# First SwiGLU of a two-layer backbone: both conditioning rows spread over the partitions by products with ones, and five column pairs streamed by row blocks instead of four plus one

## The chip, the cores and the metric

The kernel runs on one core of one Trainium2 chip. The metric is the device time of one execution in microseconds (us), as the median of several runs. The core has these engines: TensorE does matrix products (PE in the profile; PEld is its weight load), VectorE (DVE) and ScalarE (ACT) do elementwise work, GpSimd (POOL) does fills, and SyncE (SP) issues the transfers from HBM. Each engine works through its own instructions in the order that was fixed when the kernel was built, and waits on semaphores for the others.

## The reference, cut to what matters

The reference computes two layers of a diffusion backbone on 256 latent tokens and 256 context tokens, each of width 1024. What comes first, and what the change is about, is the half-step SwiGLU of layer 0, with modulation from a conditioning vector (`c` for the latent tokens, `c_ctx` for the context tokens):

```
def adaln(cond, w, b):
    mm = jax.nn.silu(cond) @ w + b
    ...
def modulate(z, g, shift, scale):
    return rmsnorm(z, g) * (1.0 + scale) + shift
def swiglu(h, wi, wo):
    a, u = jnp.split(h @ wi, 2, axis=-1)
    return (jax.nn.silu(a) * u) @ wo
x = x + 0.5 * m[2] * swiglu(modulate(x, norm_g[l, 0], m[0], m[1]), ffn1_wi[l], ffn1_wo[l])
ctx = ctx + 0.5 * mc[2] * swiglu(modulate(ctx, norm_g[l, 0], mc[0], mc[1]), ffn1_wi[l], ffn1_wo[l])
```

`wi` is 1024 x 5632, that is 22 pairs of column blocks of 128 (one block of the `a` half, one of the `u` half). All data are fp32.

## The kernel before, in words

**Two kinds of product.** Features lie on the partitions, tokens along the free axis, and the 1024 features are 8 row blocks `k`. A plain product multiplies fp32 weights with fp32 data as they come; it is recorded as two MATMUL instructions for each pair of 128x128 weights and 128x256 data. A split product (`product`, L323) takes weights and data as a high and a low part of type fp32r, and sums three cheaper MATMULs (L328, L329, L330). The split of the weights is made in `weight` (L139): a transfer into one of four buffers tagged `raw`, a copy to `hi` on ScalarE (L145), and a subtraction to `lo` on VectorE (L146).

**The start.** `run` (L532) loads the conditioning rows. The row of `c` comes as an array of 128 equal rows, 512 KB (`crow0`, L548), into `srow[0]`, and ScalarE applies Silu to it in place (L564). The row of `c_ctx` comes as a single row of 4 KB (`crow1`, L547); two products with a row of ones (L568), each of 1 partition x 128 by 1 partition x 512, spread it over the partitions in PSUM, and Silu takes it from there into `srow[1]` (L570). The small parameters come as `cols` (L550). All these are issued on SP's queue.

**The modulation vectors** are dot products on VectorE: `mod_load` (L156) brings 128 columns of `w_mod` as a 512 KB tile, and `mod_dot` (L166) multiplies it with `srow[s]` and sums along the free axis (L175), for stream `s` = 0 (latent) or 1 (context). In the start phase the tiles have names `w0` to `w7`, one buffer each.

**The streamed part.** `begin` (L602) computes the first `FIRST` = 4 pairs of column blocks for the latent tokens while the input is still arriving. `lead(k)` (L580) issues the load of `w_mod` for row block `k` and, for even `k`, 256 KB of `xT`; makes the dot product and the scale (L202); and scales the row block into `xf` on ScalarE (L588). For each `k` a 512 KB tile of `wi0k` goes into a `raw` buffer (L609), and eight plain products (L611) add into the eight PSUM banks, one for each block. `other(k)` (L598) does the same dot product for the context stream; `S1_AT` says after which `k`. ScalarE loads the table for logarithm and exponential (`log_exp_tables`, L229) after the Silus. Afterwards eight copies (L624) take the results to `early`.

**The pairs after it.** `ffn_two` (L378) goes on with pairs `nf` to 10 for the latent tokens alone. `early_weights` (L643) loads the next pair's weights; for the first `PLAIN` = 1 of these (pair 4) they stay as they are and `early_pair` (L651) uses plain products (L655), for pairs 5 to 10 they are split. `during(p)` (L627) puts the work on the context tokens beside the pairs: at `p == FIRST` the load of `ctxT` (1 MB, L630); then, two row blocks at a time, scaling (L635), squares (L636) and the split (L595, L596); at `p == FIRST + RS_AT` = 8 the inverse root mean squares of both streams (`rstd_tables`, L233, whose scratch is a `raw` buffer). The shift vectors (channel 0, 16 more dot products) are made in between by `step_mod` (L188) and finished in `second` (L660). Then pairs 0 to 10 of the context tokens follow (L421), then all the rest of the kernel.

**Order.** Each queue's order is that of the program, moved about by a list scheduler at build time, which estimates when each instruction is ready. `after` (L135) pins an instruction behind another on its engine.

Of the kernel before, what the change touches and what calls it, by code (L numbers as in the profile page):

```python
# [8 lines left out]
F32 = mybir.dt.float32  # L9
# [3 lines left out]
AF = mybir.ActivationFunctionType  # L13
ALU = mybir.AluOpType

D = 1024
# [22 lines left out]

FIRST = 4  # L40
PLAIN = 1
RS_AT = 4
S1_AT = (1, 2, 3, 4, 5, 6)
# [64 lines left out]
class Body:  # L108
# [423 lines left out]
    def run(self):  # L532
# [12 lines left out]
        self.srow = [self.t(cp, [128, D]), self.t(ap, [128, D])]  # L545
        crow = self.t(sp, [1, D])
        nc.sync.dma_start(crow, a["crow1"])  # L547
        nc.sync.dma_start(self.srow[0], a["crow0"])  # L548
        self.cols = self.t(cp, [128, NCOL])
        nc.sync.dma_start(self.cols, a["cols"])  # L550
        self.xs = [self.t(cp, [128, KB, T]), self.t(ap, [128, KB, T])]
# [11 lines left out]

        self.silu = nc.scalar.activation(self.srow[0], self.srow[0], AF.Silu)  # L564
        for i in (0, 1):
            ps = self.bank()
            c = slice(i * 512, (i + 1) * 512)
            nc.tensor.matmul(ps, row1, crow[:, c], start=True, stop=True)  # L568
            with self.after(self.silu):
                self.silu = nc.scalar.activation(self.srow[1][:, c], ps, AF.Silu)  # L570

# [30 lines left out]
        def begin(early):  # L602

            lead(0)
            tables.append(self.log_exp_tables())
            ps = [self.bank() for _ in range(2 * FIRST)]
            for k in range(KB):
                w = self.t(self.wp, [128, 1024], F32, "raw", self.raw_bufs)
                nc.sync.dma_start(w[:, :2 * FIRST * 128], a["wi0k"][k])  # L609
                for i in range(2 * FIRST):  # L610
                    nc.tensor.matmul(ps[i][:, :T], w[:, i * 128:(i + 1) * 128], xf[:, k, :],  # L611
                                     start=(k == 0), stop=(k == KB - 1))
                lead(k + 1)
                with self.after(tables[0] if k == 0 else None):
                    self.square(ss0, self.xs[0][:, k, :], k)
                if k % 2:
                    parts(Xs[0], xf, k - 1)
                if k in S1_AT:
                    other(k)
            for k in range(KB):  # L620
                if k not in S1_AT:
                    other(k)
            for i in range(2 * FIRST):
                nc.scalar.copy(early[i // 2][:, i % 2, :], ps[i][:, :T])  # L624
            return FIRST

# [16 lines left out]
        def early_weights(p):  # L643
            if p < FIRST + PLAIN:
                ws = [self.t(self.wp, [128, 1024], F32, "raw", self.raw_bufs) for _ in (0, 1)]
                for q in (0, 1):
                    nc.sync.dma_start(ws[q], a["wi0"][p, q])
                return ws
            return [self.weight(a["wi0"][p, q], 1024) for q in (0, 1)]

        def early_pair(p, ws, ps):  # L651
            for q in (0, 1):
                if p < FIRST + PLAIN:
                    for k in range(KB):
                        nc.tensor.matmul(ps[q][:, :T], ws[q][:, k * 128:(k + 1) * 128], xf[:, k, :],  # L655
                                         start=(k == 0), stop=(k == KB - 1))
                else:
                    self.product(ps[q], ws[q], Xs[0], T)

# [583 lines left out]
def _layout(x, c, ctx, c_ctx, w_mod, b_mod, norm_g, ffn1_wi, ffn1_wo, ffn2_wi, ffn2_wo, w_in, w_a2_f, b_a_f,  # L1243
# [5 lines left out]
    A["xT"], A["ctxT"] = fm(x[0]), fm(ctx[0])  # L1249
    A["crow0"] = np.broadcast_to(c, (128, D))  # L1250
    A["crow1"] = c_ctx.reshape(1, D)
    A["cols"] = np.concatenate([col(norm_g), col(b_mod), col(pool_scale), col(final_g), col(gla_g), col(b_a_f),
# [35 lines left out]
```

## Time and profile before

| | us |
|---|---|
| median of 3 runs (1151.28 to 1153.29) | 1152.44 |
| the profiled execution, whole | 1152.83 |
| its span in the trace | 1151.0 |
| TensorE busy | 1126.8 |
| VectorE busy | 932.8 |
| ScalarE busy | 585.5 |
| first block product (L611) starts at | 10.64 |

In the profile a row of the timeline gives the start, the time until the end, the engine, the line of the kernel, what is written and read, and how many instructions are merged; in brackets stands how long the engine had been idle and what ended that. In a table of windows each row gives, for a stretch of the span, its length, then for PE, PEld, DVE, ACT and POOL the busy time with the number of instructions that start in it, then the granted clock, the share of the transfer engines in use, and GB/s. Rows for SPq are issues of transfers, not the transfers themselves.

### The profile page before, as it was taken

The page shows a single profiled execution, that of the slowest core. Times are in us where ns is not written, and L with a number is a line of the kernel's source. Part 1 is how long each engine was busy: PE and PEld are TensorE (multiplying, and loading weights), DVE is VectorE, ACT ScalarE, POOL GpSimd, SP SyncE. Part 2 cuts the span into 40 slices and gives each one's busy share as a digit, 9 for nine tenths or more (in the row PEclk, how much of TensorE's full clock was granted, in tenths as well). Part 3 has the DMA queues.
Part 4 walks back from the last instruction along what each step waited for, and adds up shares of the span by engine and source line. Part 5 has one row for each costly group of instructions (what it writes and reads, how often), then busy time and mean ns, then how long its engine had stood idle before and what let it go on. Part 6 is the DMA issues. An engine that isn't in the chain of part 4 may idle for free.

```text
span 1151.0 us, 19523 instructions
## 1 busy us (share of the span) xinstructions
PE 1126.8 (98%) x7450; PEld 1020.5 (89%) x7450; DVE 932.8 (81%) x1633; ACT 585.5 (51%) x998; POOL 7.3 (1%) x30
## 2 busy tenths in 40 slices
PE   7999999999999999999999999999999999999997
PEld 5999988888888899877899998899999888988886
DVE  6899899788758788876999868899986889977664
ACT  4647645323234464665574445564444556566543
POOL 0000000000000100000000000000000000000000
PEclk9999999999999999999999999999999999999999
DMA  9867557667766535313669868868986863755562
GB/s 343 298 246 233 162 175 234 201 218 251 243 186 195 170 116 178 124 62 110 202 215 325 317 218 261 280 214 305 330 295 202 272 220 136 256 188 190 153 186 89
DMA packets 74543, 247.41 MB, mean 215 GB/s; under 512 B 8273, under 2 KB 8913, under 8 KB 74194
## 3 DMA queue, kind: packets, MB, share of 16 engines
q1 hardware_dynamic: 74450, 246.17, 64.6%
q8 instruction: 58, 0.95, 0.3%
q14 instruction: 35, 0.29, 0.1%
HBM read 245.09 MB, written 1.05 MB: 214 GB/s over the span
## 4 chain that ended last, share of the span: by engine, by line
PE 85%; DVE 8%; DMA 3%; ACT 2%; issue 1%; SPq 0%; DVEq 0%; ACTq 0%
PE t_mm L337 15%; PE t_mm L344 11%; PE t_mm L345 11%; PE t_mm L343 11%; PE t_mm L338 8%; PE t_mm L330 7%; PE t_mm L329 7%; PE t_mm L328 7%; PE t_mm L611 2%; DVE t_lo L146 2%; DVE t_junk L175 1%; ACT t_hi L145 1%; PE t_mm L991 1%; DMA t_raw<-wi0k 1%; PE t_mm L932 1%
## 5 line engine op out<-in xcount | busy, mean ns | idle before, releaser
L145 ACT CAST t_hi<-t_raw 128x1024 fp32r<-128x1024 f32 (+1 forms) x344 | 326.0, 950 | 375.3 <-PE t_mm L344 168.6
L146 DVE TENSOR_TENSOR t_lo<-t_raw,t_hi 128x1024 fp32r<-128x1024 f32 (+1 forms) x344 | 376.6, 1097 | 85.0 <-ACT t_hi L145 82.4
L330 PE MATMUL t_mm<-t_xA,t_lo 128*128 128x258 f32 (+1 forms) x912 | 259.7, 285 | 3.8 <-DVE t_lo L146 3.7
L328 PE MATMUL t_mm<-t_xA,t_hi 128*128 128x258 f32 (+1 forms) x912 | 260.0, 286 | 2.8 <-DVE t_x L953 1.7
L329 PE MATMUL t_mm<-t_xA,t_hi 128*128 128x258 f32 (+1 forms) x912 | 258.1, 283 | 0.1
L175 DVE CUSTOM_DVE_ANT_0 t_junk<-t_rawm,t_x 128x1024 bf16<-128x1024 f32 x142 | 181.7, 1280 | 25.2 <-DMA t_rawm<-wmod 24.4
L337 PE MATMUL t_mm<-t_g,t_hi 128*128 128x512 f32 x528 | 186.6, 398 | 0.0
L343 PE MATMUL t_mm<-t_xA,t_hi 128*128 128x256 f32 (+1 forms) x592 | 186.2, 315 | 0.0
L345 PE MATMUL t_mm<-t_xA,t_lo 128*128 128x256 f32 (+1 forms) x592 | 186.2, 315 | 0.0
L344 PE MATMUL t_mm<-t_xA,t_hi 128*128 128x256 f32 (+1 forms) x592 | 186.2, 315 | 0.0
L328 PEld LDWEIGHTS t_mm<-t_xA,t_hi 128*128 128x128 f32 x912 | 173.0, 190 | 7.4 <-DVE t_x L953 1.9
L330 PEld LDWEIGHTS t_mm<-t_xA,t_lo 128*128 128x128 f32 x912 | 172.7, 189 | 5.1 <-DVE t_lo L146 5.1
L329 PEld LDWEIGHTS t_mm<-t_xA,t_hi 128*128 128x128 f32 x912 | 172.7, 189 | 1.4 <-DVE t_xA L320 0.6
L338 PE MATMUL t_mm<-t_g,t_lo 128*128 128x256 f32 x528 | 148.1, 280 | 0.0
L337 PEld LDWEIGHTS t_mm<-t_g,t_hi 128*128 128x128 f32 x528 | 99.1, 188 | 23.8
L343 PEld LDWEIGHTS t_mm<-t_xA,t_hi 128*128 128x128 f32 x592 | 112.9, 191 | 6.9
L344 PEld LDWEIGHTS t_mm<-t_xA,t_hi 128*128 128x128 f32 x592 | 112.9, 191 | 6.9
L345 PEld LDWEIGHTS t_mm<-t_xA,t_lo 128*128 128x128 f32 x592 | 112.9, 191 | 6.8
L338 PEld LDWEIGHTS t_mm<-t_g,t_lo 128*128 128x128 f32 x528 | 99.7, 189 | 0.0
L337 PE MATMUL t_mm<-t_xA,t_hi 128*128 128x512 f32 x272 | 96.2, 400 | 0.0
L338 PE MATMUL t_mm<-t_xA,t_lo 128*128 128x256 f32 x272 | 75.7, 280 | 0.3 <-DVE t_lo L146 0.3
L343 PE MATMUL t_mm<-t_g,t_hi 128*128 128x512 f32 x176 | 68.5, 389 | 0.0
(244 smaller groups left out, 1351.6 us busy)
## 6 DMA issues: line engine op xcount, KB each, us to landing
t_raw<-wi SPq DMA_DIRECT2D x190, 512.0 KB, 4.6
t_rawm<-wmod SPq DMA_DIRECT2D x118, 512.0 KB, 4.6
t_raw<-wo SPq DMA_DIRECT2D x64, 384.0 KB, 3.6
t_raw<-wo SPq DMA_DIRECT2D x64, 320.0 KB, 3.3
t_raw<-win SPq DMA_DIRECT2D x18, 512.0 KB, 3.6
t_w<-wmod SPq DMA_DIRECT2D x16, 512.0 KB, 6.7
t_raw<-wmod SPq DMA_DIRECT2D x10, 512.0 KB, 4.3
t_raw<-wi0k SPq DMA_DIRECT2D x8, 512.0 KB, 6.6
```

Of the source, the lines that this page charges most:

```text
L145: nc.scalar.copy(hi[:, :n], raw[:, :n])
L146: self.mark = nc.vector.tensor_tensor(lo[:, :n], raw[:, :n], hi.bitcast(F32)[:, :n], op=ALU.subtract)
L175: self.nc.vector.tensor_tensor_reduce(out=junk, in0=w, in1=self.srow[s], scale=0.5 if half else 1.0, scalar=b, op0=ALU.mult, op1=ALU.add, ...
L328: nc.tensor.matmul(ps[:, :n], hi[:, c], X[:, 0, k, :n], start=(k == 0), stop=False)
L329: nc.tensor.matmul(ps[:, :n], hi[:, c], X[:, 1, k, :n], start=False, stop=False)
L330: nc.tensor.matmul(ps[:, :n], lo[:, c], X[:, 0, k, :n], start=False, stop=(k == KB - 1))
L337: nc.tensor.matmul(ps, hi, X.rearrange("p x t -> p (x t)"), start=first, stop=False)
L338: nc.tensor.matmul(ps[:, T:], lo, X[:, 0], start=False, stop=last)
L343: nc.tensor.matmul(ps, hi, X0, start=first, stop=False)
L344: nc.tensor.matmul(ps, hi, X1, start=False, stop=False)
L345: nc.tensor.matmul(ps, lo, X0, start=False, stop=last)
L611: nc.tensor.matmul(ps[i][:, :T], w[:, i * 128:(i + 1) * 128], xf[:, k, :], start=(k == 0), stop=(k == KB - 1))
```

## The change

The row of `c` no longer comes as 128 equal rows. Both rows come as one row of 2 x 1024 numbers (`crow`, 8 KB, one transfer), and four products with ones spread them, the first two for `srow[0]`, the last two for `srow[1]`, each followed by a Silu on ScalarE in that order. `cols` is issued on ScalarE's queue instead of SP's.

`FIRST` becomes 5 and `PLAIN` disappears: pair 4 joins the streamed part, and all pairs after it are split. The ten blocks go two to a PSUM bank, so five banks are used, and five copies of 128x512 take the results. The weights of one `k` now need two `raw` buffers: one load of 1024 columns (512 KB), one of 256 columns (128 KB). `RS_AT` becomes 3, so the inverse root mean squares stay at pair 8; the `ctxT` load moves from pair 4 to pair 5.

```diff
-FIRST = 4
-PLAIN = 1
-RS_AT = 4
+FIRST = 5
+RS_AT = 3
...
-        crow = self.t(sp, [1, D])
-        nc.sync.dma_start(crow, a["crow1"])
-        nc.sync.dma_start(self.srow[0], a["crow0"])
+        crow = self.t(sp, [1, 2 * D])
+        nc.sync.dma_start(crow, a["crow"])
         self.cols = self.t(cp, [128, NCOL])
-        nc.sync.dma_start(self.cols, a["cols"])
+        nc.scalar.dma_start(self.cols, a["cols"])
...
-        self.silu = nc.scalar.activation(self.srow[0], self.srow[0], AF.Silu)
-        for i in (0, 1):
+        self.silu = None
+        for i in range(4):
             ps = self.bank()
-            c = slice(i * 512, (i + 1) * 512)
-            nc.tensor.matmul(ps, row1, crow[:, c], start=True, stop=True)
+            nc.tensor.matmul(ps, row1, crow[:, i * 512:(i + 1) * 512], start=True, stop=True)
             with self.after(self.silu):
-                self.silu = nc.scalar.activation(self.srow[1][:, c], ps, AF.Silu)
+                self.silu = nc.scalar.activation(self.srow[i // 2][:, i % 2 * 512:i % 2 * 512 + 512], ps, AF.Silu)
...
-            ps = [self.bank() for _ in range(2 * FIRST)]
+            ps = [self.bank() for _ in range(FIRST)]
             for k in range(KB):
-                w = self.t(self.wp, [128, 1024], F32, "raw", self.raw_bufs)
-                nc.sync.dma_start(w[:, :2 * FIRST * 128], a["wi0k"][k])
+                ws = [self.t(self.wp, [128, 1024], F32, "raw", self.raw_bufs) for _ in (0, 1)]
+                nc.sync.dma_start(ws[0], a["wi0k"][k, :, :1024])
+                nc.sync.dma_start(ws[1][:, :2 * FIRST * 128 - 1024], a["wi0k"][k, :, 1024:])
+                ins = None
                 for i in range(2 * FIRST):
-                    nc.tensor.matmul(ps[i][:, :T], w[:, i * 128:(i + 1) * 128], xf[:, k, :],
-                                     start=(k == 0), stop=(k == KB - 1))
+                    with self.after(ins if k == 0 else None):
+                        ins = nc.tensor.matmul(ps[i // 2][:, i % 2 * T:i % 2 * T + T],
+                                               ws[i // 8][:, i % 8 * 128:i % 8 * 128 + 128], xf[:, k, :],
+                                               start=(k == 0 and i % 2 == 0), stop=(k == KB - 1), skip_group_check=True)
...
-            for i in range(2 * FIRST):
-                nc.scalar.copy(early[i // 2][:, i % 2, :], ps[i][:, :T])
+            for e, p in zip(early, ps):
+                nc.scalar.copy(e.rearrange("p q t -> p (q t)"), p)
...
         def early_weights(p):
-            if p < FIRST + PLAIN:
-                ws = [self.t(self.wp, [128, 1024], F32, "raw", self.raw_bufs) for _ in (0, 1)]
-                for q in (0, 1):
-                    nc.sync.dma_start(ws[q], a["wi0"][p, q])
-                return ws
             return [self.weight(a["wi0"][p, q], 1024) for q in (0, 1)]
 
         def early_pair(p, ws, ps):
             for q in (0, 1):
-                if p < FIRST + PLAIN:
-                    for k in range(KB):
-                        nc.tensor.matmul(ps[q][:, :T], ws[q][:, k * 128:(k + 1) * 128], xf[:, k, :],
-                                         start=(k == 0), stop=(k == KB - 1))
-                else:
-                    self.product(ps[q], ws[q], Xs[0], T)
+                self.product(ps[q], ws[q], Xs[0], T)
...
-    A["crow0"] = np.broadcast_to(c, (128, D))
-    A["crow1"] = c_ctx.reshape(1, D)
+    A["crow"] = np.concatenate([c.reshape(1, D), c_ctx.reshape(1, D)], 1)
```

## The prediction, made before the result was known

> **What bounds the kernel now.** First the page: who is busy, and which engine the chain runs on.
>
> ```profile
> span 1151.0 us, 19523 instructions
> PE 1126.8 (98%) x7450; PEld 1020.5 (89%) x7450; DVE 932.8 (81%) x1633; ACT 585.5 (51%) x998; POOL 7.3 (1%) x30
> PE 85%; DVE 8%; DMA 3%; ACT 2%; issue 1%; SPq 0%; DVEq 0%; ACTq 0%
> ```
>
> TensorE is the bound; 24 us of the span are without it. The change touches only the first SwiGLU's front, so the second view is the table of windows there, for where TensorE lacks work (busy columns: PE, PEld, DVE, ACT, POOL; then clock, transfer share, GB/s).
>
> ```profile
> 0.00:10.00 10.00, 3.75 (x4) 1.16 (x4) 1.69 (x4) 5.24 (x7) 0.83 (x11) 1.00 0.72 238
> 10.00:20.00 10.00, 9.36 (x36) 8.04 (x37) 7.39 (x17) 3.03 (x8) 0.00 (x0) 1.00 1.03 417
> 60.00:70.00 10.00, 10.00 (x86) 10.00 (x86) 9.14 (x13) 3.50 (x6) 0.00 (x0) 1.00 0.99 375
> 70.00:80.00 10.00, 9.85 (x69) 9.18 (x68) 9.86 (x23) 4.28 (x8) 0.16 (x2) 1.00 0.07 28
> 80.00:90.00 10.00, 9.02 (x75) 9.02 (x76) 10.00 (x13) 4.01 (x6) 0.00 (x0) 1.00 0.97 363
> ```
>
> TensorE is short of work before 10.64 us and by about one us near 80, where VectorE is full. The third view is the timeline of the start, engine by engine.
>
> ```profile
> 2.29 3.75 PE L568 MATMUL t_mm<-t_x 1*128 1x512 f32 x4 [2.29 <-DMA t_x<-crow]
> 4.78 1.06 ACT L564 ACTIVATE t_x<-t_x 128x1024 f32<-128x1024 f32 x1 [2.77 <-DMA t_x<-crow]
> 5.74 1.06 ACT L570 ACTIVATE t_x<-t_mm 128x512 f32<-128x512 f32 x2
> 6.47 1.28 DVE L175 CUSTOM_DVE_ANT_0 t_junk<-t_w,t_x 128x1024 bf16<-128x1024 f32 x1 [1.18 <-ACT t_x L570]
> 6.83 1.28 ACT L231 ACT_TABLE_LOAD   x1
> 7.80 0.16 DVE L202 SCALAR_TENSOR_TENSOR t_x<-t_x 128x1 f32<-128x1 f32 x1
> 9.35 0.51 ACT L588 ACTIVATE t_x<-t_x 128x256 f32<-128x256 f32 x1 [1.24 <-DMA t_x<-xT]
> 10.64 29.53 PE L611 MATMUL t_mm<-t_x,t_raw 128*128 128x256 f32 x128 [4.60 <-DMA t_raw<-wi0k]
> ```
>
> Two paths meet at 10.64: the conditions (Silu, dot, scale, `xf`, ready at 9.86) and the weights. The weights end last; the chain of waits and SP's timeline show their way:
>
> ```profile
> 1.14 0.35 SPq L548 DMA_DIRECT2D t_x<-crow  x1
> 2.01 0.43 SPq L163 DMA_DIRECT2D t_w<-wmod  x1
> 2.96 7.54 DMA t_raw<-wi0k
> ```
>
> **What the change leaves alone.** Streamed part and pair 4 together make 80 plain products before (64 and 16) and 80 after; pairs 5 to 10 are split in both. Their rate:
>
> ```profile
> 12.00:13.00 1.00, 1.00 (x4) 1.00 1.05 420
> 14.00:15.00 1.00, 1.00 (x6) 1.00 1.06 430
> 29.00:30.00 1.00, 1.00 (x6) 1.00 0.99 389
> L655 PE MATMUL t_mm<-t_x,t_raw x32: 379/379/379, 40.0 to 46.7; 128*128 128x256 f32 x32
> ```
>
> (In these windows for TensorE alone the x number is instructions started in one us.) The 32 of pair 4 start over 6.7 us, 0.213 us each, 0.427 a product. At 12 the rate is about half of that at 14: the first 3.4 us after 10.64 run slow although the clock column says 1.00. 128 at 0.213 are 27.3 us; 29.4 pass from 10.64 to 40.0, so this slow start costs 1.7 us and nearly nothing waits in the stream. Two products in a row into one bank cost nothing extra: L655 does that already. Copies (eight of 0.37 become five), the load of `cols` and the issues are off the path.
>
> **Term 1, the start.** Before the weights' load now go 8 KB, 512 KB of `wmod` and 256 KB of `xT`; the 512 KB `crow` is gone, and the tile is issued two slots sooner, at about 2.1 instead of 2.96. That is worth 0.9 us (the issues) to 1.4 us (512 KB at the 362 GB/s of the row below), so the weights are there at 9.1 to 9.6.
>
> ```profile
> 3.00:4.00 1.00, 1.00 (x2) 0.33 (x1) 0.00 (x0) 0.00 (x0) 0.00 (x0) 1.00 0.92 362
> ```
>
> The conditions now wait for TensorE. Two products took 3.75 us, so `srow[0]` has its second half at 6.04 plus a Silu of half of the 1.06 row, 6.7; dot and scale took 6.47 to 7.96, so the scale is ready at 8.2. But ScalarE's queue then also holds the Silus of products three and four, and perhaps the table load (1.28) ahead of the first `xf`, as it stands in the row at 6.83. The trace has no row for products three and four. Ends: at the rate of the first two they end at 9.79, at double rate at 7.9. L611 turned fast after 3.4 us of work; the ones-products would have worked 3.4 us by 5.7, so I take 7.9. Last Silu 8.5; then `xf` at 9.0 without the table load ahead, at 10.3 with it. First block product: 9.4 (the weights) or 10.35; the order is not to be seen from here, so I take 9.9 and keep both. Term: -0.75 (bounds -1.25 to +1.55, the last for slow products and the table load ahead: 9.79+0.53+1.28+0.51 = 12.1, start 12.2).
>
> **Term 2, the slow start.** If TensorE was at work until 7.9 and again from 9.9, the gap is 2.0 us instead of 4.6, and I expect the rate to stay: -1.7 (bounds -1.7 to 0). The Trainium skill, "TensorE: Matmul & The Clock Gate", Part 1, says that the clock is decided in free-running windows of about 3.4 us, full after a busy one and half after an idle one. The trace's slow 3.4 us agree. By that rule the ones-products would turn fast anywhere from 5.7 to 9.1; taking the middle they would end at 8.6, and my sum would come out 0.4 us higher.
>
> **Term 3, the seam.** Now pair 4 covers the split of pair 5's weights. Its rows:
>
> ```profile
> 36.74 0.33 SPq L144 DMA_DIRECT2D t_raw<-wi  x1
> 37.18 3.39 ACT L624 COPY t_x<-t_mm 128x256 f32<-128x256 f32 x8 [3.02 <-PE t_mm L611]
> 40.92 1.05 ACT L145 CAST t_hi<-t_raw 128x1024 fp32r<-128x1024 f32 x1 [0.34 <-DMA t_raw<-wi]
> 43.56 1.22 DVE L146 TENSOR_TENSOR t_lo<-t_raw,t_hi 128x1024 fp32r<-128x1024 f32 x1
> DMA to landing us min/median/max: 3.6/5.1/9.6
> ```
>
> (The last is for tiles `raw` up to 60 us.) That was 36.74 to 44.8, while TensorE had plain work until 46.7. Without pair 4 a `raw` buffer comes free when step 6 has done its first eight products, 12 products or 5.1 us before the stream's end E. Landing takes 3.6 at least: E-1.45. `hi` 1.05, `lo` 1.22: E+0.8 at best; the third split product needs `lo`, two cheap ones precede it, so 0.6 us of stall. If `hi` stands behind the last copy (E+0.6), `lo` ends at E+2.9, a dot product (1.28) ahead of it much the same. I take +1.6 (0.6 to 2.9). The second block's weights land 0.9 us later and are covered by the first block's products.
>
> **Term 4, the tail of the stage.** `ctxT` is issued about when the stream ends, some 6 us later against TensorE's pairs; its scaling and splitting fills ScalarE, which has 6.5 idle us in 60 to 70, so nothing is late by pair 8. The inverse roots stay at pair 8, so what follows moves along:
>
> ```profile
> 70.25 3.62 PE L241 MATMUL t_mm<-t_x 128*128 128x256 f32 x16
> 79.70 2.35 DVE L146 TENSOR_TENSOR t_lo<-t_raw,t_hi 128x1024 fp32r<-128x1024 f32 x2
> 80.98 0.39 PE L330 MATMUL t_mm<-t_xA,t_lo 128*128 128x256 f32 x1 [1.12 <-DVE t_lo L146]
> ```
>
> Pair 10 waits 1.12 us for its `lo`, which stands behind the roots on VectorE. I leave that wait as it is (0; it could go, -1.1, or grow by all that was won).
>
> **Sum.** -0.75 - 1.7 + 1.6 + 0 = -0.85. Against the profiled execution, 1152.83, that is 1152.0; it lay 0.4 above the median of the runs, so in terms of the median 1152.44 I say 1151.6.
>
> **The rivals.**
>
> *All of the gain stays.* Start at 9.4 (-1.25), rate kept (-1.7), seam at its best (+0.6), and half of pair 10's wait gone: -2.9, 1149.5. For it: every figure is a bound that a row allows. Against: the seam's best needs `hi` and `lo` each to run the moment it can, and before, `lo` began 1.6 us after `hi` had ended.
>
> *VectorE takes it back.* The 16 dot products of the shift, the `lo` parts and the roots fill VectorE from 60 to 90 (9.14, 9.86, 10.00). What TensorE is ahead by then it waits at pair 10 instead of 1.12. Result: 0, 1152.4. For it: those windows. Against: the roots follow TensorE's own pair 8, and pair 11 needs the shift only at about 86, so VectorE has slack in its order.
>
> *The ones-products hold up ScalarE* (slower). One partition's work may not raise the rate, as all four instructions before 6.04 were slow. Then the last product ends at 9.79, Silu, table load and `xf` follow on ScalarE: start 12.2, +1.55, and the slow start is paid as before; with the seam +3.15, 1155.6. It decides from a product end of about 8.9 (start 11.3), where the loss passes 2.3 us with a cold array. Against: L611 turned fast after 3.4 us.
>
> *The stream waits for its weights* (slower). Four buffers now hold two steps, not four.
>
> ```profile
> 16.02 0.33 SPq L609 DMA_DIRECT2D t_raw<-wi0k  x1
> t_raw<-wi0k SPq DMA_DIRECT2D x8, 512.0 KB, 6.6
> ```
>
> The load of step 4 went out at 16.02, when step 0 was done, and needed no haste. Now a tile goes out 5.1 us before its use, and the median landing was 6.6: six steps at 1.5 us, +9, less the 0.85, 1160.6. Against: those 6.6 us were in a full queue; now SP stands still between, and 3.6 is nearer. A step moves 1.31 MB on average, 3.1 us at 417 GB/s; even if the 1 KB rows cost as much as 4 KB ones it is 4.1 us, against 4.27 for ten products.
>
> **How the numbers follow.** A measurement of this kernel can tell about 0.2%, 2.3 us. Forecast: chance 0.38, its own range -2.2 to +1.5. All of the gain stays: 0.20. VectorE takes it back: 0.21. Ones-products: 0.15. Stream: 0.06. Faster by over 0.2%: the first rival and a tenth of the forecast, 0.24. Slower: the last two and a little of the forecast, 0.22. Same: 0.54. The range 1149.0 to 1155.8 leaves out the stream, the lower third of the first rival and the upper part of the third, 0.17 in all.
>
> **What would show it.** Right: L568 with eight instructions that end near 8, the last ones at about 0.47 us; L611 starting near 9.9 and at 0.213 from the first; 34 us for its 160; then L330 idle 1 to 3 us on L146 at the first split pair, and pair 10 waiting about 1.1. Wrong at the start if L588 waits for L231 past 11; wrong on the rate if L611 starts with half the instructions per us; wrong on the seam if no wait stands there or one over 3 us; wrong on the stream if L611 waits for `wi0k` after its first row block; wrong on the tail if pair 10's wait takes up the difference.

## The result and the profile after

The changed kernel takes 1162.67 us (median of 4 runs, 1161.98 to 1163.37) against 1152.16 for the kernel before in the same session: a ratio of 1.0086 [1.0074, 1.0099], 10.5 us slower. The prediction, 1151.6 with a range up to 1155.8, was wrong. The profiled execution took 1161.98 us. First its page:

```profile
span 1160.2 us, 19537 instructions
PE 1133.2 (98%) x7454; PEld 1022.6 (88%) x7454; DVE 933.1 (80%) x1633; ACT 586.8 (51%) x995; POOL 7.4 (1%) x30
PE 90%; DVE 5%; ACT 2%; DMA 2%; issue 1%; SPq 0%; DVEq 0%; ACTq 0%
```

TensorE has four instructions more and is busy 6.4 us longer. The two further products with ones are 3.4 of these (7.16 us for 3.75); the rest is equal work that ran slower. The timeline of the start shows the first of them, and why the block products begin later:

```profile
2.77 7.16 PE L565 MATMUL t_mm<-t_x 1*128 1x512 f32 x8 [2.77 <-DMA t_x<-crow]
1.13 1.28 ACT L275 ACT_TABLE_LOAD   x1 [1.13 <-PEq L1270]
7.36 0.42 ACT L275 ACTIVATE t_sq<-t_x 128x256 f32<-128x256 f32 x1 [4.95 <-DMA t_x<-xT]
7.80 1.28 ACT L567 ACT_TABLE_LOAD   x1
9.09 2.06 ACT L567 ACTIVATE t_x<-t_mm 128x512 f32<-128x512 f32 x4
11.18 1.28 ACT L230 ACT_TABLE_LOAD   x1
12.47 1.17 ACT L585 ACTIVATE t_x<-t_x 128x256 f32<-128x256 f32 x2
13.03 34.21 PE L611 MATMUL t_mm<-t_x,t_raw 128*128 128x256 f32 x140 [3.10 <-ACT t_x L585]
```

The eight instructions of the products with ones take 7.16 us; they start 0.85 us apart to the end, after 0.98 for the first. And on ScalarE a Square of the input (L275), which the scheduler's new order puts first, waits for its data until 7.36 us with the Silus behind it, although the first product had ended at 4.8; it also brings a table load of its own. The start comes at 13.03 us instead of 10.64.

The windows of the first 90 us, against those of the kernel before (columns as there):

```profile
0.00:10.00 10.00, 7.16 (x8) 2.49 (x8) 0.23 (x1) 3.89 (x5) 0.83 (x11) 1.00 0.77 254
10.00:20.00 10.00, 6.97 (x18) 5.64 (x19) 8.72 (x20) 5.57 (x12) 0.00 (x0) 1.00 0.51 204
80.00:90.00 10.00, 8.42 (x66) 7.90 (x65) 8.15 (x18) 5.80 (x8) 0.18 (x2) 1.00 0.34 109
18.00:19.00 1.00, 1.00 (x4) 0.82 (x3) 1.00 (x3) 0.00 (x0) 0.00 (x0) 1.00 0.00 0
20.00:21.00 1.00, 1.00 (x7) 0.87 (x6) 1.00 (x2) 0.96 (x2) 0.00 (x0) 1.00 0.32 41
```

In 10 to 20 us TensorE is busy for 6.97 us but starts only 18 instructions, and the transfers stand idle for half of the stretch. At 18 it still runs at the slow rate, at 20 at the full one; by the starts of the single instructions, 0.427 us apart and then 0.216, the change comes at 19.2. So the slow start of the array lasts some 6 us here, 3.5 before. The x number of such a window counts each instruction that lies in it in part, not those that start in it, so the prediction's "started in one us" was a misreading, though slow and full can be told apart by it.

Then SyncE's timeline and the pieces of the chain for the streamed weights, and the waits of TensorE that the kernel before does not have, or has shorter:

```profile
24.14 0.33 SPq L606 DMA_DIRECT2D t_raw<-wi0k  x1
28.45 0.33 SPq L606 DMA_DIRECT2D t_raw<-wi0k  x1
34.30 0.42 SPq L631 DMA_DIRECT2D t_x<-ctxT  x1
42.09 5.85 DMA t_raw<-wi0k
```
```profile
48.08 4.55 PE L611 MATMUL t_mm<-t_x,t_raw 128*128 128x256 f32 x20 [0.84 <-DMA t_raw<-wi0k]
54.45 0.39 PE L327 MATMUL t_mm<-t_xA,t_hi 128*128 128x256 f32 x1 [1.41 <-ACT t_hi L144]
88.01 0.39 PE L327 MATMUL t_mm<-t_xA,t_hi 128*128 128x256 f32 x1 [1.17 <-ACT t_hi L144]
88.92 0.39 PE L329 MATMUL t_mm<-t_xA,t_lo 128*128 128x256 f32 x1 [0.41 <-DVE t_lo L145]
466.10 0.39 PE L327 MATMUL t_mm<-t_xA,t_hi 128*128 128x258 f32 x1 [2.16 <-DVE t_x L944]
```

The tiles go out one step apart (24.14, 28.45), each when a buffer comes free, and the last lands 5.85 us after its issue, so that TensorE waits 0.84 us for it.

Added up to the first wide product, the first with `wo` (150.5 us before, 158.3 after, +7.8): start +2.4; the 160 instructions of the stream take 38.66 us without that wait, and 34.4 in `after_full` below, where all run at the full rate, so 4.2 are lost, where the same rate gives 1.8 for the 128 of the kernel before, +2.4; wait for weights +0.8; seam +1.4; pair 10 1.58 for 1.12, +0.5. That is 7.5. Of the 4.2 only 3.2 are the slow start, +1.4 against before. The other 1.0 is lost in short stops where steps 3, 4, 5 and 7 of the stream begin (29.3, 33.7, 38.4 and 48.1 us), too short for the views of waits or beside the 0.84; with four steps of look-ahead (`after_four_sq` below) they are gone. So the weights cost 1.8 us in the stream, not 0.8. In the mixer another 2.1 come, of which the wait there is 0.5 (2.16 for 1.69), and the rest stands in this window:

```profile
465.00:470.00 5.00, 3.90 (x20) 3.90 (x21) 3.99 (x12) 0.00 (x0) 0.00 (x0) 0.66 0.46 156
```

A granted clock of 0.66 over 5 us is 3.4 us at half speed, 1.7 us lost: from 466.5 to 469.7 us the split products start 0.21 us apart, behind that 0.12. The kernel before has one such stretch too, at 530 to 540 us (0.83 over 10 us), and the changed kernel none there, so that the spans end 9.2 us apart.

### The profile page after: what moved, and what is told of

It is laid out like the page before. It is cut to its first block, busy times and chain, and to the rows that moved or that the text cites. A ratio compares the mean times of both kernels' runs of the same rounds, so it can differ in the third digit from the quotient of the medians.

```text
span 1160.2 us, 19537 instructions
## 1 busy us (share of the span) xinstructions
PE 1133.2 (98%) x7454; PEld 1022.6 (88%) x7454; DVE 933.1 (80%) x1633; ACT 586.8 (51%) x995; POOL 7.4 (1%) x30
## 4 chain that ended last, share of the span: by engine, by line
PE 90%; DVE 5%; ACT 2%; DMA 2%; issue 1%; SPq 0%; DVEq 0%; ACTq 0%
PE t_mm L336 15%; PE t_mm L343 11%; PE t_mm L342 11%; PE t_mm L344 11%; PE t_mm L329 8%; PE t_mm L327 8%; PE t_mm L328 8%; PE t_mm L337 8%; PE t_mm L611 3%; DVE t_lo L145 1%; DMA t_raw<-wi 1%; ACT t_hi L144 1%; PE t_mm L982 1%; PE t_mm L923 1%; PE t_mm L915 1%
```

## The experiments

**Theory:** the weights of the stream, fetched two steps ahead instead of four, and the later start make the loss. **Rivals:** the start alone (ScalarE's order, products with ones); the seam; VectorE's work at pair 10. Times are medians, ratios are to the kernel before in the same session. A profile is one execution: a stretch at half speed in it, worth 1.7 us, need not be in the others of the same kernel.

| kernel | us | ratio |
|---|---|---|
| changed kernel | 1162.67 | 1.0086 [1.0074, 1.0099] |
| cond_only | 1156.4 | 1.0037 [1.0022, 1.0051] |
| stream_only | 1158.43 | 1.0051 [1.0036, 1.0065] |
| after_sq | 1163.43 | 1.0099 [1.0076, 1.0123] |
| after_four | 1157.57 | 1.0044 [1.0027, 1.0060] |
| after_four_sq | 1155.24 | 1.0024 [1.0013, 1.0035] |
| stream_four | 1154.71 | 1.0017 [1.0008, 1.0026] |
| after_ctx | 1165.11 | 1.0108 [1.0091, 1.0125] |
| after_plain5 | 1160.17 | 1.0064 [1.0045, 1.0082] |
| cond_sq | 1155.26 | 1.0018 [1.0008, 1.0028] |
| before_warm | 1153.38 | 1.0012 [1.0002, 1.0023] |
| before_warm8 | 1151.08 | 0.9987 [0.9977, 0.9996] |
| after_full | 1154.39 | 1.0019 [1.0008, 1.0029] |
| after_order | 1154.68 | 1.0019 [1.0008, 1.0031] |
| after_dots | 1164.81 | 1.0105 [1.0083, 1.0126] |
| after_full_order | 1153.22 | 1.0003 [0.9993, 1.0012] |
| after_full_order_light | 1155.1 | 1.0010 [1.0001, 1.0020] |
| after_full_order_scr | 1150.08 | 0.9976 [0.9966, 0.9987] |
| before_scr | 1151.31 | 0.9988 [0.9979, 0.9997] |

### The two halves of the change

`cond_only`: only the condition rows, on the kernel before (the diff's parts on `crow`, `cols` and the Silus).

> Four pairs streamed and pair 4 plain as before; only the condition rows are changed (one 8 KB row, four products with ones, cols on ScalarE's queue). Theory (several places share the loss, and the start is one): L611 starts near 13.0 as in the changed kernel, because the four products with ones run slowly until about 9.9 and ScalarE's queue holds a Square, two table loads and four Silus ahead of the first scaling; then a slow phase of 8 to 16 instructions; 2.4 to 4.5 us above the kernel before, and no new wait at 47 to 54. Rival (all comes from the streamed part with its two steps of buffers): the stream hides a later start, 0 to 1 us above the kernel before.

`stream_only`: only the five streamed pairs; the conditions come as before.

> Condition rows as before (512 KB of equal rows for c); five pairs streamed in two buffers a step, no plain pair after them. Theory: L611 starts near 10.6, the stream loses under 1 us to late weights, the first split pair waits 1.5 us for its hi and lo, pair 10 waits 2 us; 3 to 5 us above the kernel before. Rival (the conditions carry the loss): 0 to 1 us above. Rival (the two-step buffers carry it): over 6 us above, L611 waiting for wi0k at several steps.

Both lose, about 4 and 6 us, the stream more than the 3 to 5 expected; that they add up to about the 10.5 does not make them independent, as `after_sq` and `after_four` show. In `cond_only` the block products start at 13.00 us. In `stream_only` they start at 10.39 and then wait twice for weights, as the timeline shows:

```profile
25.94 13.30 PE L613 MATMUL t_mm<-t_x,t_raw 128*128 128x256 f32 x60 [0.40 <-DMA t_raw<-wi0k]
40.45 8.87 PE L613 MATMUL t_mm<-t_x,t_raw 128*128 128x256 f32 x40 [1.21 <-DMA t_raw<-wi0k]
```

Both also have a longer wait at pair 10, with a half-speed window behind it (0.83 over 80 to 90 us).

### The stream: start against look-ahead

`after_sq`: all Squares stay behind the table of logarithms.

```diff
-                with self.after(tables[0] if k == 0 else None):
+                with self.after(tables[0]):
                     self.square(ss0, self.xs[0][:, k, :], k)
```

> The changed kernel, with all Squares of the latent tokens pinned behind the second table load, so that none stands ahead of the Silus. Theory (the four slow products with ones bound the start): Silus end at 10.5 instead of 11.15, first scaling right after them, L611 at 11.1 to 12.3 instead of 13.03, so 0.7 to 1.9 us below the changed kernel. Rival (the hoisted Square with its table load is the whole loss of the start): L611 back at 10.6, 2.4 us or more below.

The start moves from 13.03 to 11.01, and nothing is won: the first split product comes at 52.7 us, as in the changed kernel (52.5), because the stream now waits 0.44 and 2.17 us for weights and runs at half speed behind the second wait. At pair 10 TensorE waits 2.92 us and the clock falls:

```profile
26.88 13.19 PE L611 MATMUL t_mm<-t_x,t_raw 128*128 128x256 f32 x60 [0.44 <-DMA t_raw<-wi0k]
42.23 10.56 PE L611 MATMUL t_mm<-t_x,t_raw 128*128 128x256 f32 x40 [2.17 <-DMA t_raw<-wi0k]
91.42 0.58 PE L329 MATMUL t_mm<-t_xA,t_lo 128*128 128x256 f32 x1 [2.92 <-DVE t_lo L145]
```
```profile
90.00:95.00 5.00, 3.58 (x16) 3.58 (x17) 5.00 (x7) 1.04 (x1) 0.00 (x0) 0.56 0.90 286
```

`after_four_sq`: the same, and the narrow tile of each step lies in a part of `early` that is not used yet, so that four `raw` buffers are four steps.

```diff
-                ws = [self.t(self.wp, [128, 1024], F32, "raw", self.raw_bufs) for _ in (0, 1)]
+                ws = [self.t(self.wp, [128, 1024], F32, "raw", self.raw_bufs), early[FIRST + k // 2][:, k % 2, :]]
```

> The changed kernel with two edits: the narrow weight tile of each streamed step goes into the not yet used part of early, so that all four raw buffers hold wide tiles and four steps of weights can be on their way instead of two; and the Squares stay behind the table of logarithms on ScalarE, as in the run before that moved the start to 11.0 without any gain. Theory (the weights, fetched two steps ahead, set the end of the streamed part): the waits for wi0k go, and the streamed part, which starts at 11.0, ends 2 to 4 us earlier: the first split product starts at 48.5 to 50.5 us instead of 52.5; the time falls to 1158 to 1161 us, less than that gain, because the wait at pair 10 grows when TensorE arrives there earlier. Rival (the look-ahead is slack, and something else, the context tokens' input or VectorE, sets 52.5): the first split product stays at 52 to 53 us and the time at 1162 to 1164 us.

From 1163.43 to 1155.24 us, more than was expected. The view of TensorE's waits up to 100 us has no wait for `wi0k`, and no seam either:

```profile
PE t_mm L565 <- DMA t_x<-crow: 2.6, 1, 2.6
PE t_mm L329 <- DVE t_lo L145: 1.3, 1, 1.3
PE t_mm L611 <- ACT t_x L585: 1.1, 1, 1.1
```

The first split product starts at 48.1 us, 4.6 earlier, and the first wide product at 151.7 instead of 163.5. So the look-ahead is worth far more than the 2.6 us of waits that name the weights: with it go the seam (the casts of the next pair's weights come early enough), 2.5 us of waiting at pair 10, and three half-speed windows (clock 0.83 over 40 to 50 us, 0.66 over 90 to 100 in `after_sq`; 1.00 in both stretches here).

`after_four`: the look-ahead alone, with the Square where the change puts it.

> The changed kernel with the look-ahead of four steps alone; the Square stays ahead of the Silus on ScalarE, so that the block products start at 13.0 us again, not at 10.9. Theory (with the weights there in time, the start counts in full): no wait for wi0k, the first split product at 49.5 to 51 us, and 2 us more than with both edits: 1156.5 to 1158.5 us. Rival (the start still has slack behind the weights or VectorE): the first split product at 48 to 48.6 and 1155 to 1156 us.

1157.57 us, start at 13.03, first split product at 49.3. Once the weights are there, the later start counts: about 2 us, where without look-ahead it counted for nothing.

`stream_four`: the look-ahead in `stream_only`.

> The streamed part of five pairs with conditions as in the kernel before (1158.4 us with two steps of look-ahead), and four steps of look-ahead. Theory (the look-ahead was all that the streamed part lost): no wait for wi0k, the block products from 10.4 us on, the first split product at 46.8 to 48 us as in the kernel before, and 1152 to 1154 us. Rival (five pairs in one stream cost something of their own, by the two blocks to a bank or the missing plain pair): 1155.5 us or more.

1154.71 instead of 1158.43 us; no wait for weights after the first. That lies between the theory and the rival. The stream of five pairs has no large cost of its own; what stays against the kernel before, 1.0017 or some 2 us, agrees with a first split product 1.9 us later (48.6 us), of which 0.5 are a later start (11.11, the first weights) and the rest a longer slow phase.

`after_ctx`: the changed kernel with `ctxT` pinned behind the last streamed weights.

```diff
-                nc.sync.dma_start(self.xs[1], a["ctxT"])
+                with self.after(self.last):
+                    nc.sync.dma_start(self.xs[1], a["ctxT"])
```

> The changed kernel, but the 1 MB load of the context tokens is pinned behind the last load of streamed weights on SyncE's queue. Theory (these 1 MB go ahead of the weights of the last two steps, which are waited for, 0.84 us, at 48.1): that wait goes, the first split product starts 0.5 to 1 us earlier, at 51.5 to 52 us, and the time is 1161 to 1162 us. Rival (the weights are late because their two buffers come free late, whatever is on the queue): the wait of 0.5 us or more stays, and with it 52.5 us and 1162.5 us. Third possibility: the context tokens come too late for their own work beside the pairs, and pair 10 pays for it: 1163 us or more.

The guess falls: the wait at the last step is gone, but two others, 1.3 us together, stand at earlier steps, the first split product comes at 53.4 us, and pair 10 waits 3 us, with the clock at 0.66. So the 1 MB ahead in the queue is not what makes the weights late; that it is the freeing of the buffers is shown by `after_four` and `after_four_sq`. The 1165.11 us and the longer wait at pair 10 are what the third possibility had, late context tokens; no run here tells whether they are the cause.

`after_plain5`: pair 5 with plain products, as pair 4 had before.

> The changed kernel, but pair 5, the first after the streamed part, has plain products from raw weights as pair 4 had in the kernel before. Theory (the seam costs what TensorE waits there for hi and lo of the first split pair, 0.4 + 1.4 us): these waits go, the plain pair costs 1.2 us more than a split one, and the roots start at 76.0 to 76.5 us instead of 76.9; the time is 1161.5 to 1163 us, hardly another. Rival (the seam is the main loss of the change): the time falls by 3 us or more, to 1159.5 us or less.

1160.17 us, 2.5 less than the changed kernel, between the theory and the rival. The profile does not show so much: the roots start at 76.1 us instead of 76.9. The waits of the seam are gone, but the stream waits 1.51 us for weights instead of 0.84, so this run does not price the seam alone. It is no main loss.

### The start

`cond_sq`: `cond_only` with the Squares pinned.

> The condition rows of the change on the kernel before (1156.4 us), with the Squares behind the table on ScalarE. Theory (the Square ahead of the Silus, with its table load, made the start late): the block products start at 11.0 us instead of 13.0, the first split product at 47 us instead of 49.1, the wait at pair 10 falls and the clock there stays at 1.00, and the time is 1152 to 1154 us. Rival (the four products with ones and four Silus themselves are the loss, or the dot products at pair 10): the start is 11.0, but the time stays at 1155.5 to 1157 us.

The start is 11.10 us instead of 13.00, but the time falls only from 1156.4 to 1155.26: pair 10 waits 0.38 + 2.33 us with a half-speed window behind it, much as the rival had it. Of the 1.9 us of earlier start, 0.9 are left at the first wide product (154.4 us against 155.3).

`before_warm` and `before_warm8`: the kernel before with products of 128x128 ones that nobody reads, 5 ahead of the products with ones and 20 behind, or 8 behind.

```diff
+        for _ in range(8):
+            with self.after(mm):
+                nc.tensor.matmul(pw[:, :128], self.ones, self.ones, start=True, stop=True)
```

> The kernel before, with 5 extra products of 128x128 ones ahead of the two products with ones and 20 behind them, whose results nobody reads, so that TensorE works with the full array from 1 to about 10.4 us. Theory (the slow phase at the start of L611 is an array that was idle): L611 runs at 0.213 us an instruction from the first or nearly so, 1.0 to 1.7 us below the kernel before. Rival (the slow phase comes from elsewhere, or the extra products push L611 later): the same or up to 1 us above.

> The kernel before with eight products of 128x128 ones behind the two products with ones, which write to a bank that nobody reads; they fill the time in which TensorE waits for the first scaled row block. Theory (the slow start of the array is a term of its own, 1.7 us in the kernel before): the block products start at 10.6 us as before, reach full speed 2 to 3.5 us earlier than at 14.1, the first split product starts at 45 to 46 us instead of 46.7, and the time is 1150.6 to 1151.5 us against 1152.3. Rival (an earlier TensorE waits longer at pair 10): the first split product is as early, the wait at pair 10 grows by as much, and the time stays at 1152 to 1152.6 us, or rises if the clock drops there.

In `before_warm` the added products are themselves slow from 7.1 to 12.2 us and too many, so the block products start at 14.03, but at full speed from the first; 1153.38 us, as the rival had it. In `before_warm8` they are slow too (5.95 to 9.73 us, 16 instructions 0.21 us apart, where those of `before_warm` end 0.11 apart), and after 1.13 us without work the block products begin slowly all the same; the first split product is at 47.3 us, not earlier. The 1.5 us that it gains by the medians are not explained by this theory. In its profile TensorE is 1.8 us behind the kernel before until 534 us and 1.3 ahead at 583; between them the kernel before has its half-speed stretch and two waits for `lo` (0.77 and 0.48 us) that are missing here.

`after_full`: `after_four_sq`, but the products with ones have 128 partitions: one row of numbers, 127 of zeros.

```diff
-        crow = self.t(sp, [1, 2 * D])
-        nc.sync.dma_start(crow, a["crow"])
+        crow = self.t(sp, [128, 2 * D])
+        nc.vector.memset(crow[:, :D], 0.0)
+        nc.gpsimd.memset(crow[:, D:], 0.0)
+        nc.sync.dma_start(crow[0:1, :], a["crow"])
...
-        row1 = self.t(sp, [1, 128])
+        row1 = self.t(sp, [128, 128])
```

> The kernel with the look-ahead of four steps and the Squares behind the table, in which the products with ones have 128 partitions instead of one: the row of numbers is the first of 128 rows, the others are filled with zeros, at the cost of a fill ahead of the load. Theory (one partition is not work enough to raise TensorE's clock; 128 are): the products with ones start at 3.5 to 4.5 us, the first of their eight instructions take 0.9 us and the last 0.45, the block products run at 0.22 us an instruction from the first or the second microsecond on, and the first split product starts at 45.5 to 47 us instead of 48.1; the time falls to 1153 to 1154.5 us. Rival (the array starts slow whatever ran before it, or one partition counts as much as 128): all eight take 0.9 us, the block products are slow for 3 to 6 us again, and the time is 1155 to 1157 us, as the fill and the load are later.

This tells it apart. The view of the line gives the durations (ns, least/median/most), the timeline the start:

```profile
L567 PE MATMUL t_mm<-t_x x8: 592/755/1192, 5.1 to 9.8; 128*128 128x512 f32 x8
```
```profile
5.05 5.33 PE L567 MATMUL t_mm<-t_x 128*128 128x512 f32 x8 [5.05 <-DVE t_x L560]
11.46 3.72 PE L613 MATMUL t_mm<-t_x,t_raw 128*128 128x256 f32 x16 [1.08 <-ACT t_x L587]
```

The same products go from 1192 to 592 ns, and the first 16 instructions of the block products take 3.72 us, where they took 6.46 in `after_four_sq`. With one partition all eight were 1056 ns or more. The first split product starts at 45.9 us, 2.2 earlier in spite of a later load; yet the time falls by 0.9 us only, which the intervals cannot tell from nothing.

`after_order`: `after_four_sq` with the context row's two Silus behind the first `xf`.

> The kernel with the look-ahead of four steps and the Squares behind the table, in which ScalarE makes the two Silus of the context row after the first scaling of xf instead of before it. Theory (the start is ScalarE's order and then the four products with ones): the first block product starts at 9.8 to 10.0 us, when the fourth product with ones ends, instead of 10.9, and the time falls by 1 us to 1153.8 to 1154.8 us. Rival (the wait at pair 10 takes it back, and may cost the clock): the start is as early, the wait there grows from 1.3 to over 2 us, and the time stays at 1155 us or rises to 1157.

Start at 9.87 us as expected, first wide product at 150.9 instead of 151.7, and 1154.68 us: not to be told from 1155.24.

### Pair 10

`after_dots`: the last shift products pinned behind the roots on VectorE, 1.8 of them a pair instead of 1.2.

> The changed kernel, but the last dot products of the shift vectors are pinned behind the roots on VectorE, and more of them are made beside the pairs (1.8 for each pair instead of 1.2). Theory (at pair 10 TensorE waits because these dot products stand ahead of the roots on VectorE, ScalarE's logarithm waits for the roots' first step, and the casts of the weights stand behind the logarithm on ScalarE): the waits of 1.2 and 0.4 us at pair 10 fall under 0.3 us together, no window there has a granted clock under 0.95, and the first wide product starts 1 to 3 us earlier than 158.3; the time is 1159 to 1161.5 us. Rival (the weights themselves are late there, because the roots' scratch holds a raw buffer): the waits stay over 1 us, and the time at 1162 to 1164 us.

The waits at pair 10 shrink to 0.5 us, so the order on VectorE does count there, but the time does not fall: the context pairs now wait for the shift itself, the clock drops with it, and the kernel takes 1164.81 us:

```profile
PE t_mm L327 <- DVE t_xA L313: 2.8, 1, 2.8
```

`after_full_order`: look-ahead, pinned Squares, full-height products and the order of `after_order` together.

> All repairs of the changed kernel together: look-ahead of four steps, Squares behind the table, full-height products with ones, and the two Silus of the context row behind the first scaling of xf. Theory (pair 10's wait behind VectorE's dot products takes an earlier start back): the block products start at 10.3 to 10.6 us at full speed and the first split product at 44.8 to 45.3 us, 1 us earlier than with three of the repairs, but the wait at pair 10 grows by about 1 us and the first wide product stays at 150 to 150.8 us: 1153 to 1155 us, or 1.7 more if the clock falls there. Rival (an earlier start counts): the first wide product at 149.2 to 149.6 us, 1152.5 to 1153.5 us.

1153.22 us, level with the kernel before (1.0003 [0.9993, 1.0012]). The start was not the hoped-for 10.4 us but 11.73, because the load behind the fills came later and the products with ones ran until 11.26. Pair 10 waits:

```profile
80.63 0.39 PE L329 MATMUL t_mm<-t_xA,t_lo 128*128 128x256 f32 x1 [1.57 <-DVE t_lo L145]
```

`after_full_order_light`: the same without half of the shift's dot products; zeros stand for their results.

```diff
-            self.need_mod(0, 0)
+            self.units = [u for u in self.units if u[1]]
+            for m in skip:
+                nc.gpsimd.memset(m, 0.0)
...
+        self.units = self.units[:4]
+        skip = [self.mod_tile(0, 0, s)[:, 4:8] for s in (0, 1)]
```

> The kernel with all four repairs, in which half of the dot products of the shift vectors (8 of 16, with their 2 MB of weights) are left out, and zeros stand for their results. Theory (these dot products on VectorE make TensorE wait at pair 10): the wait of 1.5 to 2.5 us there falls under 0.4 us, the first wide product starts 1.5 to 2.5 us earlier than with all of them, and the time is 1150 to 1152.5 us. Rival (the weights, by the raw buffer that the roots hold, make the wait): it stays over 1 us, and the time within 0.5 us of the kernel with all of them.

The theory falls; the time is 1155.1 us. With 8 dot products gone VectorE is idle for 6.58 us ahead of the roots, and TensorE still waits 1.17 + 0.41 us at pair 10; the first line is VectorE's timeline, the second TensorE's:

```profile
72.69 0.69 DVE L247 TENSOR_SCALAR t_raw<-t_mm 128x512 f32<-128x512 f32 x1 [6.58 <-PE t_mm L240]
79.69 0.39 PE L327 MATMUL t_mm<-t_xA,t_hi 128*128 128x256 f32 x1 [1.17 <-ACT t_hi L144]
```
```profile
80.00:85.00 5.00, 4.59 (x26) 4.39 (x25) 5.00 (x6) 1.57 (x2) 0.00 (x0) 0.66 0.86 283
```

The half-speed stretch in this window is 1.7 of the 1.9 us by which it is slower than `after_full_order`.

`after_full_order_scr` and `before_scr`: the roots' scratch in the tiles of `early` that pairs 9 and 10 fill later, instead of a `raw` buffer.

```diff
-                    spare = self.t(self.wp, [128, 1024], F32, "raw", self.raw_bufs)
+                    spare = self.early_t
...
+            self.early_t = early
...
-            v, w = [spare[:, i * ns * T:(i + 1) * ns * T].rearrange("p (s t) -> p s t", t=T) for i in (0, 1)]
+            v, w = [spare[NP // 2 - 2 + i] for i in (0, 1)]
```

> The changed kernel with all four repairs, in which the roots' scratch lies in the tiles of early that pairs 9 and 10 fill later, not in a raw buffer. All dot products are made. Theory (the raw buffer held by the roots makes the weights late at pair 10): the wait of 1.6 us there falls under 0.5 us, the first wide product starts 1 to 2 us earlier than 150.1, and the time is 1150.5 to 1152.3 us, below the kernel before. Rival (the casts are late behind the logarithm and VectorE's work, whatever buffer the scratch has): the wait stays over 1 us, and the time at 1152.5 to 1154 us.

> The kernel before with the roots' scratch in the tiles of early that pairs 9 and 10 fill later, and nothing else. Theory: its wait of 1.1 us at pair 10 falls under 0.4 us, the first wide product starts 0.8 to 1.2 us earlier than 150.5, and the time is 1 us lower, 1151.3 to 1152.2 us. Rival: the wait stays at 1 us or more, and the time within 0.4 us of the kernel before.

Here the wait goes. In the first, TensorE has no wait at all between the conditions' load and 160 us; this is the window in which the run without the move is busy for 4.37 us:

```profile
80.00:85.00 5.00, 5.00 (x45) 5.00 (x44) 5.00 (x13) 2.65 (x5) 0.22 (x2) 1.00 0.34 96
```

The first wide product starts at 148.3 us instead of 150.1, and the time is 1150.08 us, 0.9976 [0.9966, 0.9987] of the kernel before: the version that beats both. That is 3.1 us less than `after_full_order` by the medians; what goes beyond the 1.8 lies behind 150 us, where the profile of `after_full_order` has a half-speed stretch at 532 us and this one has none. In `before_scr` the wait at pair 10 is gone too, and it is 1.4 us faster by the medians. The earlier first wide product that was expected did not come in its profile (150.6 us against 150.5), as its first split product was 1.4 us later than in the kernel before (48.1); behind it, its profile lacks the half-speed stretch at 532 us.

What the move changes is ScalarE's order. Two rows of the kernel before, then two of `before_scr`, in which the roots' logarithm begins at 77.21 us:

```profile
75.51 0.63 ACT L249 ACTIVATE t_rs<-t_raw 128x512 f32<-128x512 f32 x1 [5.12 <-DVE t_raw L248]
76.99 2.00 ACT L145 CAST t_hi<-t_raw 128x1024 fp32r<-128x1024 f32 x2
```
```profile
68.64 1.05 ACT L145 CAST t_hi<-t_raw 128x1024 fp32r<-128x1024 f32 x1 [1.50 <-PE t_mm L329]
71.46 1.05 ACT L145 CAST t_hi<-t_raw 128x1024 fp32r<-128x1024 f32 x1 [1.50 <-PE t_mm L329]
```

These are the casts of pair 10's weights. In the kernel before, the weights were issued at 62.70 and 63.84 us and landed 6.8 us later, at 69.5 and 70.7, but the casts stand behind the logarithm, ahead of which ScalarE is idle for 5.12 us. So the weights are not late, though the expectations call them so; with the scratch in a `raw` buffer their casts are ordered behind the roots, and without it ahead of them. Why the scheduler orders them so is not shown.

## Why the prediction was wrong, point by point

**Term 1, the start (-0.75), failed: +2.4.** Two steps of it. "So I take 7.9" let the products with ones turn fast after 3.4 us of work; all eight stayed at 0.85 us from start to start, and they ended at 9.9. `after_full` shows the reason: with one partition the array does not speed up, with 128 it does. And ScalarE's order was read from the old trace: the Square went ahead of the Silus. `after_sq` shows that the Square made 2.0 us of the start (13.03 against 11.01); the slow products made the rest.

**Term 2, the slow start (-1.7), failed: the stream lost 2.4 more.** It hung on the same step, that the products with ones count as work. The array was cold at 13.03 and stayed so for some 6 us. That is 3.2 us lost for 1.8, +1.4; the other 1.0 of the term's +2.4 are short stops for weights, which belong to the rival with the stream. The phase lasted between 3.5 us (the kernel before) and 7.4 (`stream_four`), for the same kind of work. The prediction's own difference for the kernel before, 29.4 less 27.3, is 2.1 and not 1.7; with the full rate of `after_full` it is 1.8.

**Term 3, the seam (+1.6), held in size only: 1.4.** The prediction had TensorE wait for `lo` of the pair's first block and held the second block's weights to be covered. But TensorE waited until 54.45 for a cast to `hi` on ScalarE, the second of the pair, which ran from 53.33 to 54.39; that the sizes agree is luck. And it is no property of the missing plain pair: with four steps of look-ahead it is gone (`after_four_sq`), as the next weights' buffers then come free earlier.

**Term 4, the tail (0), was +0.5 in the changed kernel, and its reason was only half of it.** Pair 10's `lo` does stand behind the roots on VectorE, and its `hi` behind the logarithm on ScalarE. But half of the dot products that fill VectorE can be left out without any gain; both casts move ahead when the roots' scratch leaves the `raw` buffers. Its price is also no fixed 1.1 us: with the scratch in a `raw` buffer it was 0.5 (`after_dots`) to 3.8 (`after_sq`), with up to 3.4 us more for half-speed windows.

**The rival with the weights named the mechanism and had 0.06.** It was set aside because "3.6 is nearer" than the median landing of 6.6; in the changed kernel the tiles of 512 KB took 5.5 us in the median of the page, and the one issued at 42.09 was wanted at 47.24, 5.15 later. Its direct price was overrated (1.5 us in each of six steps; the waits came to 0.2 to 2.6 in all, in the changed kernel to 1.8 with the short stops), and what follows from a wait was left out: the seam, pair 10 and the clock. In all the look-ahead was worth 5.1 us by the medians with the start of the change, 8.2 with the earlier one.

**The rival with the products with ones had the slow products and the cold array rightly**, with a start at 12.2 for 13.03, and lacked the Square. Both rivals came true together; the prediction had treated them as alternatives, and as unlikely ones.

What stays open: 2 us in the mixer, where the wait grew from 1.69 to 2.16 us and a half-speed window came with it, why `before_warm8` is faster, and why a half-speed stretch follows one short wait and not another.

## What to carry to other kernels

Before taking buffers from a stream for wider tiles, compare the time from the freeing of a buffer to its next use (here 5.15 us) with the landing time under load (5.5), not with the fastest one; then an earlier start is worth nothing until that is mended. Any edit at the front makes the scheduler order the queues anew: read the new order of each engine before counting on the old one, above all where a table load or a wait for data can slip ahead of the critical chain. Scratch space that is taken from a stream's buffers can hold up that stream; look for space that is dead at that moment. And read the order on each engine before calling a wait late weights: here they had landed.

## What the runs showed of the hardware

Products with one partition followed each other 0.85 us apart for 7.16 us (1056 ns each, as they overlap) and did not speed up the array; with 128 partitions the same products fell from 1192 to 592 ns within 5.3 us. The granted-clock column reads 1.00 through the slow start, so the slow start is seen only in the rates.

Short waits can cost more than their length. 1.17 + 0.41 us at pair 10 left the clock at 1.00 in the changed kernel (85 to 90 us) and were followed by 0.66 over 5 us in `after_full_order_light`; 0.47 us at 532.7 in the kernel before was followed by 0.83 over 10 us, and the same wait at 542.6 in the changed kernel by none. Each such stretch is 3.4 us at half speed, 1.7 us lost. The Trainium skill, "TensorE: Matmul & The Clock Gate", Part 1, says that the clock is decided by free-running windows of about 3.4 us; the length agrees, and so does it that the same wait costs nothing or 1.7 us by where it falls. The Trainium skill's table of the two states gives an idle window of that length as what leads to half speed; here 19 of the 20 stretches that the profiles show between 40 and 540 us begin within a wait of 0.5 to 2.9 us or up to 1.5 us behind it, and these waits are well under 3.4. That the waits cause them is argued from where they stand; no run here shows it alone.
